# Output stage of a two-layer diffusion trunk: one buffer for each block's input, scaled ahead, and the gate row transposed ahead of the first products

## The chip, the core and the metric

The kernel runs on one core of one Trainium2 chip. The core has four engines that compute, TensorE (PE, matrix products and transposes), VectorE (DVE), ScalarE (ACT) and GpSimd (POOL), and a queue of SyncE (SP) from which this kernel issues its transfers. Each engine takes its instructions strictly in the order of its own queue and waits at one whose inputs or buffers are not ready. The metric is the time of one execution on the device in microseconds.

## The reference

Two post-norm layers run over 1024 latent tokens of width 1024, with 256 context tokens that share the weights. The first layer is windowed attention with sinks, the second neighbourhood attention on a 64-wide grid. Both end alike, and only the end of the second layer, for the latent tokens, is touched here:

```python
    y = (o * jax.nn.silu(g)) @ w_out
    ...
        h = layer_norm(DEEPNORM_ALPHA * h + gate[:, None, :] * y, ln_g[i], ln_b[i])
```

So for each token the attention output times its gate path goes through a 1024 x 1024 matrix; the row is multiplied by `gate` (one vector of 1024 for all tokens), added to the scaled input of the layer, and normalised over its 1024 values with weights `ln_g` and `ln_b`.

## The kernel before

Matrix products are made in three passes to keep float32 accuracy: each operand is split into a high and a low part, and high x high, high x low and low x high are summed (`out_part`, lines 451 to 453).

The output stage works through eight blocks of 128 tokens. A block's product has 8 steps of depth (`KT`) and two halves of 512 columns, each in a bank of PSUM of its own (`psone`, four banks in turn), so 48 products of 128x128 by 128x512. Blocks 0 and 1 have only their last step left when the stage begins: the first seven were put between the attention's last pieces of work. The last step uses `o7`, the output of the last head pair, which is ready only when the attention ends. The other seven steps read `og`, which the attention wrote to device memory and which is loaded again in four transfers a block (line 395, one buffer of three, two blocks ahead). Block 7 has its second half cut in two quarters, so that less is left to do behind the last product.

The layer's input was left in device memory by the first layer, normalised but without its weights (`zdd`). For each block `x` is loaded from it (line 1336, one buffer of three), and GpSimd multiplies it by `vecs[0]` (line 1340) and adds `vecs[1]` (line 1341): the first layer's `ln_g` and `ln_b`, each times ALPHA, made by GpSimd at the start of the stage (line 1331).

For each half of a block VectorE then multiplies the product by the gate row `g1` (line 1355, which also empties the PSUM bank), adds `x` (line 1356) and takes statistics (line 1357). For the block it combines them (line 459) and adds the epsilon (line 460); GpSimd raises that to the power -1/2 (line 461, one value per token); VectorE subtracts the mean and multiplies by `ln_g` (line 1362), then scales by the result of line 461 and adds `ln_b` (line 1364), and SP stores the block (line 1365). `z`, in which all this happens, has three buffers.

The gate row `g1` is needed in every partition. It lies as eight columns in `dcol`; `gate_rows` broadcasts and transposes them on TensorE (line 377, eight transposes) and copies the result out of PSUM on ScalarE (line 378). It is called once, behind block 0's products.

The order on each engine is not written by hand here. The kernel is written as a program, and a planner plays it through with costs of its own when it is built: an engine that is free takes, among the instructions whose inputs are ready by then, the one that stands first in the program. An instruction written later can so pass one that is written earlier but is not ready in the planner's reckoning. The order is then fixed; the chip's own times no longer change it. The planner also places the buffers. The output stage's buffers lie on memory that the attention used before, and each transfer into one waits until the attention's last use of that place.

Of the kernel before, what the change touches and what calls it, by code (L numbers as in the profile page):

```python
# [11 lines left out]
F32 = mybir.dt.float32  # L12
# [3 lines left out]
ALU = mybir.AluOpType  # L16
# [3 lines left out]
P = 128  # L20
D = 1024
# [61 lines left out]
def build(tc, i, out):  # L83
    nc = tc.nc
    mm = nc.tensor.matmul
    dma = nc.sync.dma_start
    es = ExitStack()

    def pool(name, side="left", **kw):
        st = ExitStack()  # L90
        p = st.enter_context(tc.tile_pool(name=name, bufs=1, side=side, reuse_waits="tile", **kw))
        return p, st
# [4 lines left out]
    def psbig(name):  # L97
        return ps.tile([P, 1024], F32, tag="big", bufs=2, name=name)

    def psone(name):  # L100
        return ps.tile([P, 512], F32, tag="one", bufs=4, name=name)
# [10 lines left out]
    dcol = cp.tile([P, 32, 2], F32, name="dcol")  # L112
# [8 lines left out]
    zdd = dr.tile([S, D], F32, name="zdd")  # L121
# [251 lines left out]
    def gate_rows(dst, src):  # L373

        pg = psbig("gate")
        for j in range(KT):
            nc.tensor.transpose(pg[:, j * P : (j + 1) * P], src[:, j : j + 1].to_broadcast([P, P]), ident)
        nc.scalar.copy(dst, pg)
# [9 lines left out]
    def ogs_load(b, alloc):  # L388

        o = []  # L390
        for k0 in range(0, KT - 1, 4):
            n = min(4, KT - 1 - k0)
            t = alloc(k0 // 4, n)
            for x in range(2):
                dma(f32(t[x]), ogs[k0 : k0 + n, x, :, b * P : (b + 1) * P].rearrange("k p t -> p k t"))
            o += [(t[0][:, k], t[1][:, k]) for k in range(n)]
        return o

    def og_home(pl, tag, bufs=1):

        t = pl.tile([P, 2, KT - 1, P], F32R, tag=tag, bufs=bufs, name="og")
        return lambda k, n: [t[:, x, 4 * k : 4 * k + n] for x in range(2)]
# [35 lines left out]
    def part_of(y, sl):  # L438

        if len(y) == 3 and sl.start == 768:  # L440
            return y[2][:, : sl.stop - sl.start]
        nh, c = sl.start // 512, sl.start // 512 * 512
        return y[nh][:, sl.start - c : sl.stop - c]

    def out_part(y, sl, o, w, kts):

        yy = part_of(y, sl)
        for kt in kts:
            h, l = o[kt]
            wh, wl = w.at(kt, sl)  # L450
            mm(yy, h, wh, start=kt == 0, stop=False)
            mm(yy, h, wl, start=False, stop=False)
            mm(yy, l, wh, start=False, stop=kt == KT - 1)

    def ln_stats(pl, st):

        mv = pl.tile([P, 2], F32, tag="mv", bufs=2, name="mv")
        rs = pl.tile([P, 2], F32, tag="rsd", bufs=2, name="rsd")
        nc.vector.bn_aggr(mv, st)  # L459
        nc.vector.tensor_scalar(rs[:, 0:1], mv[:, 1:2], EPS, None, ALU.add)  # L460
        nc.gpsimd.tensor_tensor(rs[:, 1:2], rs[:, 0:1], half, ALU.pow)  # L461
        return mv, rs
# [810 lines left out]
    def grid_rows(t, b):  # L1273

        return t.rearrange("(r c) d -> r c d", c=64)[:, 8 * b : 8 * b + 8, :]
# [49 lines left out]
    ob, ob_st = pool("outB", "left")  # L1325
    vecs = []
    for j in range(4):
# [3 lines left out]
            nc.gpsimd.tensor_scalar(t, t, ALPHA, 0.0, ALU.mult, ALU.add)  # L1331
        vecs.append(t)
    parts_of = {0: o0, 1: o1}
    for b in range(8):
        x = ob.tile([P, D], F32, tag="x", bufs=3, name="x")
        dma(x, grid_rows(zdd, b))  # L1336
        tok = slice(b * P, (b + 1) * P)
        if b < 6:
            parts_of[b + 2] = ogs_load(b + 2, og_home(ob, "og", 3))
        nc.gpsimd.tensor_tensor(x, x, vecs[0], ALU.mult)  # L1340
        nc.gpsimd.tensor_tensor(x, x, vecs[1], ALU.add)  # L1341
        y = [y0, y1][b] if b < 2 else [psone(f"yB{b}_{nh}") for nh in range(3 if b == 7 else 2)]
        pairs = parts_of.pop(b) + [(o7[:, 0, tok], o7[:, 1, tok])]

        cuts = (0, 512, 768, 1024) if b == 7 else (0, 512, D)
        parts = [slice(*c) for c in zip(cuts, cuts[1:])]
        for sl in parts:
            out_part(y, sl, pairs, woB, range(KT) if b > 1 else (KT - 1,))
        if b == 0:
            g1 = ob.tile([P, D], F32, name="g1")  # L1350
            gate_rows(g1, dcol[:, 24:32, 0])
        z = ob.tile([P, D], F32, tag="z", bufs=3, name="z")
        st = ob.tile([P, 3, 6], F32, tag="stat", bufs=2, name="stat")
        for j, sl in enumerate(parts):
            nc.vector.tensor_tensor(z[:, sl], part_of(y, sl), g1[:, sl], ALU.mult)  # L1355
            nc.vector.tensor_tensor(z[:, sl], z[:, sl], x[:, sl], ALU.add)  # L1356
            nc.vector.bn_stats(st[:, j, :], z[:, sl])  # L1357
        mv, rs = ln_stats(ob, st[:, : len(parts)])
        cuts = (0, 512, 1024) if b == 7 else (0, D)
        parts = [slice(*c) for c in zip(cuts, cuts[1:])]  # L1360
        for sl in parts:
            nc.vector.scalar_tensor_tensor(z[:, sl], z[:, sl], mv[:, 0:1], vecs[2][:, sl], ALU.subtract, ALU.mult)  # L1362
        for sl in parts:
            nc.vector.scalar_tensor_tensor(z[:, sl], z[:, sl], rs[:, 1:2], vecs[3][:, sl], ALU.mult, ALU.add)  # L1364
            dma(grid_rows(out, b)[:, :, sl], z[:, sl])
# [97 lines left out]
```

## Time and profile before

| what | us |
|---|---|
| median of 3 runs | 1425.7 (1424.68 to 1426.22) |
| profiled execution, its own time | 1422.99 |
| its span in the trace | 1421.2 |
| first L1355 of the output stage | 1341.86 |
| last product ends | 1410.30 |
| last L1364 ends | 1417.26 |

Times in the rows are microseconds from the span's start. A row of a queue gives the start, the duration, the engine, the line of the kernel, the operation, what is written from what (buffer numbers left out), shapes, and in brackets the idle time before it and what ended that. `xN` joins N instructions in sequence, and the duration is then that of all of them. A row of a group gives the number of instructions, then the sum in us, the mean in ns, and the idle time ahead. "SPq" is the queue of the transfers: its rows show the issuing, not the moving of the data.

### The profile page before, as it was taken

How to read it: one execution, taken by the hardware profiler on the slowest of the kernel's cores; microseconds unless marked ns; L12 is line 12 of the kernel's file. 1: busy time of each engine (PE TensorE's matmuls, PEld its weight loads, DVE VectorE, ACT ScalarE, POOL GpSimd, SP SyncE). 2: the span in 40 equal slices, each digit the busy share in tenths (PEclk: the TensorE clock that was granted, in tenths of full speed). 3: DMA queues.
4: the chain of work that ended last, by engine and by line, in shares of the span. 5: the costliest groups of instructions: out<-in, count | busy, mean ns of one | idle time of the engine just before them, and what ended most of it. 6: DMA issues, size and time to landing. Idle time of an engine off the chain costs nothing. (4 is left out here: it accounts for less than half of the span.)

```text
span 1421.2 us, 25164 instructions
## 1 busy us (share of the span) xinstructions
PE 1385.3 (97%) x8816; PEld 1215.2 (86%) x8816; DVE 980.0 (69%) x2220; ACT 731.4 (51%) x1560; POOL 626.2 (44%) x776
## 2 busy tenths in 40 slices
PE   8999999999999999999999999999999999999996
PEld 6988898888988888888898899888998899888885
DVE  4658887878888789566433766566665564659598
ACT  4337776676776778432222555454454454558200
POOL 0326676667666567233211333332233232325583
PEclk9999999999999999999999999999999999999998
DMA  9572114123222114443187575564555564476753
GB/s 377 181 224 85 54 57 126 53 79 92 79 73 64 57 60 146 127 135 133 62 260 218 156 214 165 143 189 137 179 150 172 150 185 146 137 209 185 181 149 107
DMA packets 128141, 202.39 MB, mean 142 GB/s; under 512 B 9744, under 2 KB 66448, under 8 KB 128016
## 3 DMA queue, kind: packets, MB, share of 16 engines
q1 hardware_dynamic: 127872, 200.78, 47.0%
q8 instruction: 70, 1.15, 0.3%
q14 instruction: 55, 0.45, 0.1%
q10 hardware_dynamic: 144, 0.01, 0.0%
HBM read 145.18 MB, written 55.57 MB: 141 GB/s over the span
## 5 line engine op out<-in xcount | busy, mean ns | idle before, releaser
L334 POOL TENSOR_SCALAR s_B<-s_B,rs_B 128x640 f32<-128x640 f32 (+1 forms) x128 | 103.2, 806 | 289.8 <-DVE rs_B L333 262.7
L212 PE MATMUL pj<-uBh,wh 128*128 128x512 f32 (+1 forms) x448 | 175.9, 393 | 0.0
L213 PE MATMUL pj<-uBl,wh 128*128 128x512 f32 (+1 forms) x448 | 170.3, 380 | 0.0
L214 PE MATMUL pj<-uBh,wl 128*128 128x512 f32 (+1 forms) x448 | 170.1, 380 | 0.0
L329 ACT ACTIVATE s_B<-s_B,m_B 128x640 f32<-128x640 f32 (+1 forms) x128 | 102.9, 804 | 126.1 <-DVE m_B L322 125.9
L329 ACT ACTIVATE s_A<-s_A,m_A 128x641 f32<-128x641 f32 (+2 forms) x160 | 119.5, 747 | 82.9 <-DVE m_A L322 60.1
L168 POOL TENSOR_TENSOR wl<-wr,wh 128x512 fp32r<-128x512 f32 x65 | 88.2, 1358 | 158.1 <-ACT wh L163 146.4
L334 POOL TENSOR_SCALAR s_A<-s_A,rs_A 128x640 f32<-128x640 f32 (+2 forms) x160 | 128.8, 805 | 65.0 <-DVE rs_A L333 58.9
L322 DVE CUSTOM_DVE_ANT_0 s_A<-S_A,msk,nsk 128x640 f32<-128x640 f32 (+2 forms) x160 | 123.5, 774 | 32.3 <-PE S_A L755 18.2
L347 DVE TENSOR_TENSOR pt_B<-T_B,pt_B 128x640 fp32r<-128x640 f32 (+1 forms) x128 | 100.9, 788 | 60.2 <-ACT pt_B L345 59.7
L212 PE MATMUL pj<-uAh,wh 128*128 128x512 f32 (+1 forms) x384 | 140.2, 365 | 0.8 <-DVE otmp L794 0.8
L213 PE MATMUL pj<-uAl,wh 128*128 128x512 f32 (+1 forms) x384 | 137.6, 358 | 0.0
L214 PE MATMUL pj<-uAh,wl 128*128 128x512 f32 (+1 forms) x384 | 137.2, 357 | 0.0
L347 DVE TENSOR_TENSOR ptl_A<-T_A,pth_A 128x640 fp32r<-128x640 f32 (+2 forms) x160 | 114.1, 713 | 16.8 <-PE pvA L783 10.5
L341 PE MATMUL T_A<-ident,s_A 128*128 128x128 f32 x672 | 100.9, 275 | 10.7 <-DVE m_A L322 5.3
L345 ACT CAST pt_B<-T_B 128x640 fp32r<-128x640 f32 (+1 forms) x128 | 84.4, 659 | 48.2 <-PE T_B L341 47.2
L341 PEld LDWEIGHTS T_A<-ident,s_A 128*128 128x128 f32 x672 | 77.3, 140 | 37.0 <-issue 10.1
L322 DVE CUSTOM_DVE_ANT_0 s_B<-S_B,bias 128x640 f32<-128x640 f32 (+1 forms) x128 | 100.2, 783 | 8.0 <-PE S_B L1092 7.0
L345 ACT CAST pth_A<-T_A 128x640 fp32r<-128x640 f32 (+2 forms) x160 | 96.3, 602 | 17.2 <-PE T_A L341 15.7
L214 PEld LDWEIGHTS pj<-uBh,wl 128*128 128x128 f32 x448 | 84.3, 188 | 16.6
L213 PEld LDWEIGHTS pj<-uBl,wh 128*128 128x128 f32 x448 | 84.7, 189 | 9.1
L341 PE MATMUL T_B<-ident,s_B 128*128 128x128 f32 x608 | 88.1, 274 | 4.2 <-DVE pt_B L347 2.3
(224 smaller groups left out, 3866.8 us busy)
## 6 DMA issues: line engine op xcount, KB each, us to landing
kB<-kdB SPq DMA_DIRECT2D x64, 320.0 KB, 5.4
gw<-in_wadaT SPq DMA_DIRECT2D x48, 256.0 KB, 2.8
vdB<-st SPq DMA_DIRECT2D x20, 512.0 KB, 3.6
vB<-vdB SPq DMA_DIRECT2D x16, 640.0 KB, 4.6
wada<-in_wadaC SPq DMA_DIRECT2D x16, 512.0 KB, 9.6
kdB<-st SPq DMA_DIRECT2D x16, 512.0 KB, 2.8
qdB<-st SPq DMA_DIRECT2D x16, 512.0 KB, 3.7
qB<-qdB SPq DMA_DIRECT2D x32, 256.0 KB, 4.8
```

The source lines that it names most:

```text
L168: e.tensor_tensor(lo, r, f32(hi), ALU.subtract)
L212: mm(pt[:, :n], hi[:, sl], rh, start=kt == 0, stop=False)
L213: mm(pt[:, :n], hi[:, sl], rl, start=False, stop=False)
L214: mm(pt[:, :n], lo[:, sl], rh, start=False, stop=kt == KT - 1)
L322: nc.vector.tensor_tensor_reduce(outp, sc, in1, scale, init if init is not None else 3e38, ALU.add, ALU.min, accum_out=s.m)
L329: nc.scalar.activation(s.t[:, :n], s.t[:, :n], AF.Exp, bias=s.m, scale=-1.0, accum_out=s.sum)
L334: nc.gpsimd.tensor_scalar(s.t[:, : s.w], s.t[:, : s.w], s.rs, 1.0, ALU.mult, ALU.mult)
L341: nc.tensor.transpose(tp[:, k * P : (k + 1) * P], s.t[:, src * P : (src + 1) * P], ident)
L345: nc.scalar.copy(pt.hi[:, :n, hl, :], tv)
L347: nc.vector.tensor_tensor(pt.lo[:, :n, hl, :], tv, f32(pt.hi[:, :n, hl, :]), ALU.subtract)
```

## The change

The eight `x` get a buffer each (32 KB a partition in place of 12). Loading and scaling are put in a function, `x_make`, which is called once ahead of block 0's `og` load, twice behind it, twice more in block 1, and once in each of blocks 2, 3 and 4. The loads of `x` no longer wait for a buffer, and in the program's order an `x` stands two or three blocks ahead of its use. The call of `gate_rows` moves from behind block 0's products to ahead of them.

```diff
     parts_of = {0: o0, 1: o1}
+    xs = []
+
+    def x_make():
+        x = ob.tile([P, D], F32, name=f"x{len(xs)}")
+        dma(x, grid_rows(zdd, len(xs)))
+        nc.gpsimd.tensor_tensor(x, x, vecs[0], ALU.mult)
+        nc.gpsimd.tensor_tensor(x, x, vecs[1], ALU.add)
+        xs.append(x)
+
     for b in range(8):
-        x = ob.tile([P, D], F32, tag="x", bufs=3, name="x")
-        dma(x, grid_rows(zdd, b))
         tok = slice(b * P, (b + 1) * P)
+        if b == 0:
+            x_make()
         if b < 6:
             parts_of[b + 2] = ogs_load(b + 2, og_home(ob, "og", 3))
-        nc.gpsimd.tensor_tensor(x, x, vecs[0], ALU.mult)
-        nc.gpsimd.tensor_tensor(x, x, vecs[1], ALU.add)
+        for _ in range(2 if b in (0, 1) else 1 if len(xs) < 8 else 0):
+            x_make()
+        x = xs[b]
...
+        if b == 0:
+
+            g1 = ob.tile([P, D], F32, name="g1")
+            gate_rows(g1, dcol[:, 24:32, 0])
         for sl in parts:
             out_part(y, sl, pairs, woB, range(KT) if b > 1 else (KT - 1,))
-        if b == 0:
-            g1 = ob.tile([P, D], F32, name="g1")
-            gate_rows(g1, dcol[:, 24:32, 0])
```

More of the change, by code (lines that the diff above doesn't have):

```diff
@@ L1346, in build @@
         parts = [slice(*c) for c in zip(cuts, cuts[1:])]
-        for sl in parts:
-            out_part(y, sl, pairs, woB, range(KT) if b > 1 else (KT - 1,))
         if b == 0:
@@ L1351, in build @@
             gate_rows(g1, dcol[:, 24:32, 0])
+        for sl in parts:
+            out_part(y, sl, pairs, woB, range(KT) if b > 1 else (KT - 1,))
         z = ob.tile([P, D], F32, tag="z", bufs=3, name="z")
```

## The prediction

> **What bounds the kernel now.** I read the head of the page first, then the groups of the last 80 us by form, then the queues of POOL, DVE, PE and SP in order of time.
>
> ```profile
> span 1421.2 us, 25164 instructions
> PE 1385.3 (97%) x8816; PEld 1215.2 (86%) x8816; DVE 980.0 (69%) x2220; ACT 731.4 (51%) x1560; POOL 626.2 (44%) x776
> ```
>
> PE is busy for 97% of the whole, but the change touches only the output stage, and there the end is set by another engine. These are rows of VectorE (start, duration, then the instruction):
>
> ```profile
> 1341.86 1.29 DVE L1355 TENSOR_TENSOR z<-yB,g 128x512 f32<-128x512 f32 x2 [10.04 <-ACT g L378]
> 1348.61 0.14 DVE L460 TENSOR_SCALAR rsd<-mv 128x1 f32<-128x1 f32 x1
> 1382.75 0.68 DVE L1355 TENSOR_TENSOR z<-yB,g 128x512 f32<-128x512 f32 x1
> 1392.74 0.68 DVE L1355 TENSOR_TENSOR z<-yB,g 128x512 f32<-128x512 f32 x1
> 1402.08 0.68 DVE L1355 TENSOR_TENSOR z<-yB,g 128x512 f32<-128x512 f32 x1
> 1409.53 0.69 DVE L1355 TENSOR_TENSOR z<-yB,g 128x512 f32<-128x512 f32 x1
> 1412.83 0.41 DVE L1355 TENSOR_TENSOR z<-yB,g 128x256 f32<-128x256 f32 x1
> 1415.85 1.41 DVE L1364 SCALAR_TENSOR_TENSOR z<-z,rsd,vec 128x512 f32<-128x512 f32 x2
> ```
>
> The first row is block 0. The next L1355 rows open blocks 4, 5, 6 and 7: block 4 takes 9.99 us, block 5 9.34, block 6 only 7.45. Now PE over the same stretch:
>
> ```profile
> 1338.35 0.40 PE L451 MATMUL yB<-woBh,o 128*128 128x512 f32 x1
> 1339.74 1.04 PE L377 MATMUL gate<-ident,dcol 128*128 128x128 f32 x8
> 1340.53 0.49 PE L451 MATMUL yB<-woBh,o 128*128 128x512 f32 x1
> 1342.61 0.50 PE L451 MATMUL yB<-woBh,og 128*128 128x512 f32 x1 [0.42 <-DVE z L1355]
> 1387.60 0.39 PE L451 MATMUL yB<-woBh,og 128*128 128x512 f32 x1
> 1410.02 0.28 PE L453 MATMUL yB<-woBh,o 128*128 128x256 f32 x1
> ```
>
> The last product ends at 1410.30, but VectorE takes it up only at 1412.83. So VectorE is **2.5 us behind** PE at the end and bounds the stage; if it kept up, the end would come at most 2.5 us earlier, and PE's own 0.42 us wait at 1342.61 (with 0.1 us in the longer product behind it) gives 0.5 more. **3.0 us is the most that anything here can win.**
>
> Why VectorE is behind is seen in its two-input instructions (ns: min/median/max):
>
> ```profile
> L1356 DVE TENSOR_TENSOR z<-z,x x17: 425/693/2884, 1343.1 to 1413.3; 128x512 f32<-128x512 f32 x15, 128x256 f32<-128x256 f32 x2
> L1362 DVE SCALAR_TENSOR_TENSOR z<-z,mv,vec x9: 740/1275/2269, 1348.7 to 1415.2; 128x1024 f32<-128x1024 f32 x7, 128x512 f32<-128x512 f32 x2
> L1364 DVE SCALAR_TENSOR_TENSOR z<-z,rsd,vec x9: 743/1285/3412, 1350.5 to 1416.5; 128x1024 f32<-128x1024 f32 x7, 128x512 f32<-128x512 f32 x2
> L1356 DVE TENSOR_TENSOR z<-z,x 128x512 f32<-128x512 f32 x15 | 21.1, 1413 | 0.3
> L1364 DVE SCALAR_TENSOR_TENSOR z<-z,rsd,vec 128x1024 f32<-128x1024 f32 x7 | 15.2, 2175 | 1.8 <-POOL rsd L461 1.8
> L1362 DVE SCALAR_TENSOR_TENSOR z<-z,mv,vec 128x1024 f32<-128x1024 f32 x7 | 10.9, 1557 | 0.0
> ```
>
> Mean against median: 15 x 0.72 + 7 x 0.89 + 7 x 0.28 = **19.0 us of stretching**. And POOL's queue shows with whom it collides:
>
> ```profile
> 1332.71 2.41 POOL L1340 TENSOR_TENSOR x<-x,vec 128x1024 f32<-128x1024 f32 x1
> 1335.19 2.40 POOL L1341 TENSOR_TENSOR x<-x,vec 128x1024 f32<-128x1024 f32 x1
> 1340.22 2.38 POOL L1340 TENSOR_TENSOR x<-x,vec 128x1024 f32<-128x1024 f32 x1 [2.64 <-DMA x<-zdd]
> 1342.68 2.40 POOL L1341 TENSOR_TENSOR x<-x,vec 128x1024 f32<-128x1024 f32 x1
> 1349.17 1.19 POOL L461 TENSOR_TENSOR rsd<-rsd,half 128x1 f32<-128x1 f32 x1 [4.09 <-PE yB L453]
> 1352.87 3.27 POOL L1341 TENSOR_TENSOR x<-x,vec 128x1024 f32<-128x1024 f32 x1
> 1356.10 2.86 POOL L1340 TENSOR_TENSOR x<-x,vec 128x1024 f32<-128x1024 f32 x1
> 1360.37 1.53 POOL L461 TENSOR_TENSOR rsd<-rsd,half 128x1 f32<-128x1 f32 x1 [1.41 <-DVE rsd L460]
> 1371.14 3.26 POOL L1341 TENSOR_TENSOR x<-x,vec 128x1024 f32<-128x1024 f32 x1
> 1374.36 2.85 POOL L1340 TENSOR_TENSOR x<-x,vec 128x1024 f32<-128x1024 f32 x1
> 1377.29 2.73 POOL L1341 TENSOR_TENSOR x<-x,vec 128x1024 f32<-128x1024 f32 x1
> 1379.99 1.53 POOL L461 TENSOR_TENSOR rsd<-rsd,half 128x1 f32<-128x1 f32 x1
> 1396.62 2.72 POOL L1341 TENSOR_TENSOR x<-x,vec 128x1024 f32<-128x1024 f32 x1
> ```
>
> L1340 is the multiply and L1341 the add on one x; L461 is the reciprocal root of a block, for which L1364 waits. Alone an x instruction takes 2.40 us; back to back beside VectorE it takes 2.7 to 3.3. From block 0's start to the add of x7 (1396.62), 13 x instructions run beside VectorE; 19.0 / 13 = 1.46 us of stretching each. Block 6, with none beside it, shows the bare 7.45 us.
>
> **The change, part by part.** (1) *The gate row.* The eight transposes move ahead of block 0's six products. Those took 1339.74 - 1338.35 = 1.39 us, so g and the first L1355 come 1.4 us earlier. But L1356 behind it needs the path that POOL occupies: at 1341.66 it meets x1's multiply (until 1342.60) and then its add, and the second L1356 ends near 1346.1, as now. Bounds 0 and -1.4; I take **-0.2**, since those rows of POOL stay where they are. PE's 0.5 us is gained but hidden while VectorE is the bound.
>
> (2) *The x loads.* SP's queue: two issues, two of its waits (us in total, times, longest), and the stretch from 1325 to 1342, whose last figure is GB/s:
>
> ```profile
> 1331.85 2.01 SPq L395 DMA_DIRECT2D og<-ogdB  x4
> 1333.90 0.54 SPq L1336 DMA_DIRECT2D x<-zdd  x1
> SPq L395 <- DVE o L1159: 8.8, 1, 8.8
> SPq L1336 <- DVE z L1356: 7.0, 3, 4.1
> 1325.00:1342.00 17.00, 17.00 (x89) 14.16 (x88) 2.97 (x6) 3.46 (x7) 11.94 (x10) 1.00 0.80 217
> ```
>
> With eight buffers the 7.0 us of waiting for an L1356 goes, and x3 to x7 are loaded without it. x2 passes four og transfers, and x3, x4 pass og of block 4. Up to that og SP moves three og of 0.92 MB and four x of 0.52 (by their shapes), 4.8 MB; at 217 GB/s that is 22 us from 1331.85, so 1354. Block 4 starts two blocks behind 1342.61; a block is 48 products at 0.232 us (six from 1338.35 to 1339.74), 11.1 us, so 1365. Covered by the products of blocks 2 and 3, cost 0; without those 11 us PE would wait that long. The larger pool lies on more of the attention's memory: og waits 8.8 us for its last instruction now, and x1 queues behind it. If x1 came free of this, it could be scaled at 1337.6 instead of 1340.22, and one instruction fewer would collide (-1.46); if another x takes over the place, nothing changes. Bounds -1.5 and 0; I take 0.
>
> (3) *POOL's order.* The instructions are the same sixteen. What moves is where they stand against the four or five early L461. x1 already goes ahead of block 0's L461, though written behind it, because it was loaded; x3's multiply goes ahead of block 1's, x4 and x5 ahead of block 3's. With every x loaded early, two more will stand ahead of each. POOL works in order, so L461 waits, and VectorE waits at L1364 with all its later work behind it.
>
> I follow POOL from the end of x1's add, 1345.08. x2's multiply ends at 1347.5; block 0's L461 (ready at 1348.75) ends at about 1350.0. Ahead of block 3's L461 then stand x2's add, x3 to x6 (8), none, one or both instructions of x7, and two L461 at 1.53. An x instruction back to back costs the mean of the five such rows (3.27, 2.86, 3.26, 2.85, 2.73: 2.99) and a gap of 0.08, **3.1 us**; bounds are 2.48 (alone, 1332.71 to 1335.19) and 2.40 + 1.28 = 3.7 (an L1364 in each gap). At 3.1, block 3's L461 starts at 1350.0 + 3.1 + (27.9, 31.0 or 34.1 less 3.1) + 3.1 = 1381.0, 1384.1 or 1387.2, against 1379.99 now: **1.0, 4.1 or 7.2 us late**. Afterwards blocks 4 and 5 run with fewer x beside them. They lie 2.54 and 1.89 above the bare 7.45, 4.4 together, 1.1 for each of their four x instructions. With two, one or none left, 2.2, 3.3 or 4.4 come back. The ends move by -1.2, +0.8 or +2.8, and with the gate row by **-1.4, +0.6 or +2.6**.
>
> Here a rule of the Trainium skill can be weighed (SBUF — State Buffer, "Who interferes with whom"): VectorE with two SBUF inputs and a GpSimd instruction that reads SBUF shut each other out for a whole instruction. The rows agree in kind (L1364 up to 3412 ns against 1285). Taken at its worst the rule gives an estimate of 12 x 2.40 = 28.8 us of waiting in place of 19.0, so +9.8; the rows say that VectorE spends part of each POOL instruction on L1355 and L1357, which are not stretched, and 1.46 us is left, so the rule's worst gets no chance of its own.
>
> I choose the middle one. In the trace an L461 falls between the two instructions of an x (x3 at block 1), and x7 is the last in the order of the program.
>
> The sum is made against the profiled execution, 1422.99 us, 1.79 above its span; the median of the runs shown is 1425.7, 2.7 above it. 1422.99 + 0.6 = 1423.6; against the median **1426.3**.
>
> **The rivals.**
>
> *VectorE catches up.* x1 free early, each L461 between two x, x instructions nearer 2.5 us: then VectorE is through with the collisions by block 4, takes the last product at once, and PE bounds. That gives the full 3.0: **1422.7**. For it: blocks 5 to 7 have no x at all beside them. Against: the number of collisions falls only from 13 to 12, and VectorE has no idle time in which to absorb them before block 4.
>
> *L461 behind all of x7* (the slower side). Place: block 3's L461. Its price: 11 instructions at the longest row, 3.27 + 0.08, are 36.9; 1350.0 + 36.9 + 3.1 = 1390.0, 10 us late; less 4.4 and 0.2, +5.4: **1431.1**. It decides from the point at which more comes late than blocks 4 and 5 give back, 4.4 us; nearly the same lateness (1387.60 - 1383.43 = 4.2 us for block 4's first half) is where PE starts to wait for the bank that L1355 empties. For it: x4 and x5 stand both ahead of block 3's L461 already. Against: x7's loads are the last ones.
>
> *The order of POOL hardly changes*, because the loads arrive as late as now (SP keeps 0.5 MB transfers behind og and the outputs). Then the gate row alone is left, -0.2: **1425.5**. Against: the wait for L1356 is named in the queue, and it goes.
>
> **How the numbers follow.** A measurement of this kernel can tell about 0.2% (2.9 us) from no change. Chances: the forecast with its two neighbours (1424.3 to 1428.3) 0.60; VectorE catches up 0.13; L461 behind all of x7 0.19; the order hardly changes 0.08. The 3.0 us limit leaves little room below 1422.9, and I cut the range there; the slow case is let in to 1429.6, about half of it. The likeliest case's own range is 1424.3 to 1428.3. Faster by over 0.2%: 0.13, nearly all of the first rival. Slower: 0.24, the second rival and the upper edge of the forecast. Within: 0.63.
>
> **What would show it.** Right: no "DMA x<-zdd" wait of L1340 after x2; x7's add ends before 1392 (now 1399.34); block 3's L1364 comes later than 1381.55, behind an L461 that starts the moment an x instruction ends; blocks 5 and 6 both at 7.4 to 7.5 us; stretching still 17 to 20 us in all. The gate row: L377 ahead of 1338.35 in PE's order, and no wait at the first product of block 2. Wrong, if VectorE's last L1355 follows the last product within 0.3 us (the first rival), if PE waits more than 1 us for L1355 (the second), or if the stretching falls below 14 us: then the collisions went and were not only moved.

## The result, and the profile after

The changed kernel takes **1426.8 us** (median of 22 runs, 1425.05 to 1429.81) against 1424.33 us for the kernel before (22 runs beside them, 1423.24 to 1427.15). The ratio is **1.0015, with an interval of 1.0009 to 1.0021**: 2.1 us slower (1.3 to 3.0), which is a real difference, but within the 0.2% that the prediction called no change. The prediction was 1426.3 us, 0.6 above before.

The profiled execution took 1425.88 us, its span 1424.1. A note for all that follows: the profiled execution of the kernel before (1422.99 us) is 1.3 us faster than its median of 1424.33, so a comparison with its trace can make another kernel look slower by up to that much. Verdicts come from the ratios, mechanisms from the traces.

VectorE's three two-input groups after the change (sum in us, mean in ns, then the idle time ahead):

```profile
L1368 DVE TENSOR_TENSOR z<-z,x 128x512 f32<-128x512 f32 x15 | 19.0, 1272 | 0.3
L1376 DVE SCALAR_TENSOR_TENSOR z<-z,rsd,vec 128x1024 f32<-128x1024 f32 x7 | 17.3, 2474 | 7.0 <-POOL rsd L461 7.0
L1374 DVE SCALAR_TENSOR_TENSOR z<-z,mv,vec 128x1024 f32<-128x1024 f32 x7 | 10.3, 1470 | 0.0
```

L1368, L1376 and L1374 are the L1356, L1364 and L1362 of before; L1367 is L1355, and L1377 the store. The stretching is hardly changed, but the wait for L461, 1.8 us before, is now 7.0. Where it lies is seen in VectorE's queue:

```profile
1330.45 0.94 DVE L1159 TENSOR_TENSOR o<-gB,o 128x256 fp32r<-128x256 f32 x1 [1.35 <-ACT o L1156]
1340.04 1.89 DVE L1367 TENSOR_TENSOR z<-yB,g 128x512 f32<-128x512 f32 x3 [8.65 <-ACT g L378]
...
1378.40 1.27 DVE L1374 SCALAR_TENSOR_TENSOR z<-z,mv,vec 128x1024 f32<-128x1024 f32 x1
1385.32 3.39 DVE L1376 SCALAR_TENSOR_TENSOR z<-z,rsd,vec 128x1024 f32<-128x1024 f32 x1 [5.64 <-POOL rsd L461]
1388.63 0.68 DVE L1367 TENSOR_TENSOR z<-yB,g 128x512 f32<-128x512 f32 x1
...
1397.52 0.68 DVE L1367 TENSOR_TENSOR z<-yB,g 128x512 f32<-128x512 f32 x1
...
1404.97 0.69 DVE L1367 TENSOR_TENSOR z<-yB,g 128x512 f32<-128x512 f32 x1
...
1412.42 0.69 DVE L1367 TENSOR_TENSOR z<-yB,g 128x512 f32<-128x512 f32 x1
...
1415.73 0.41 DVE L1367 TENSOR_TENSOR z<-yB,g 128x256 f32<-128x256 f32 x1
...
1418.75 1.41 DVE L1376 SCALAR_TENSOR_TENSOR z<-z,rsd,vec 128x512 f32<-128x512 f32 x2
```

Two rows of the kernel before belong beside these, its last L1159 and the L1364 of its block 3:

```profile
1330.88 0.95 DVE L1159 TENSOR_TENSOR o<-gB,o 128x256 fp32r<-128x256 f32 x1 [1.35 <-ACT o L1156]
...
1381.55 1.28 DVE L1364 SCALAR_TENSOR_TENSOR z<-z,rsd,vec 128x1024 f32<-128x1024 f32 x1 [0.44 <-POOL rsd L461]
```

I measure the stage from the end of the last L1159 to the end of the last long instruction. It took 1417.26 - 1331.83 = 85.43 us before and 1420.16 - 1331.39 = **88.77** after, 3.3 more. The account, block by block:

- The first product is taken up 1.4 us earlier (8.65 us of waiting in place of 10.04).
- In block 3 VectorE waits 5.64 us for L461 (0.44 before), and the L1376 behind it takes 3.39 us (1.28 before): +5.2 and +2.1. The rest up to block 4 adds 0.4. So block 4 begins 1388.63 - 1331.39 = 57.24 us into the stage in place of 50.92, **6.3 late**.
- Block 4 takes 8.89 us (9.99 before) and block 5 takes 7.45 (9.34): 3.0 come back. Blocks 6 and 7 are as before.

6.3 - 3.0 = 3.3. Now POOL, for whose L461 block 3 waits:

```profile
1369.01 2.39 POOL L1340 TENSOR_TENSOR x<-x,vec 128x1024 f32<-128x1024 f32 x1
1371.48 3.25 POOL L1341 TENSOR_TENSOR x<-x,vec 128x1024 f32<-128x1024 f32 x1
1379.93 2.38 POOL L1340 TENSOR_TENSOR x<-x,vec 128x1024 f32<-128x1024 f32 x1 [5.20 <-DMA x<-zdd]
1382.39 2.39 POOL L1341 TENSOR_TENSOR x<-x,vec 128x1024 f32<-128x1024 f32 x1
1384.74 0.55 POOL L461 TENSOR_TENSOR rsd<-rsd,half 128x1 f32<-128x1 f32 x1
1385.25 2.38 POOL L1340 TENSOR_TENSOR x<-x,vec 128x1024 f32<-128x1024 f32 x1
1387.71 3.23 POOL L1341 TENSOR_TENSOR x<-x,vec 128x1024 f32<-128x1024 f32 x1
```

These are x5, x6, block 3's L461 and x7. POOL stood 5.20 us at x6, whose data had not come, with block 3's small L461 queued behind it; it then scaled x6 and only at 1384.74 took the L461. In SP's queue x6's load is the third row, behind the store of block 2, which waits for that block's last instruction:

```profile
1366.39 3.62 SPq L395 DMA_DIRECT2D og<-ogdB  x4
1372.51 0.58 SPq L1377 DMA_DIRECT2D out_h<-z  x1
1373.13 0.60 SPq L1339 DMA_DIRECT2D x<-zdd  x1
```

And PE, with the view of one stretch behind it (its length, then busy time and number of instructions of PE, PEld, DVE, ACT and POOL, PE's granted clock, DMA share, GB/s):

```profile
1386.24 0.40 PE L453 MATMUL yB<-woBh,o 128*128 128x512 f32 x1
1389.37 0.50 PE L451 MATMUL yB<-woBh,og 128*128 128x512 f32 x1 [2.73 <-DVE z L1367]
...
1390.62 0.63 PE L452 MATMUL yB<-woBl,og 128*128 128x512 f32 x1
1391.05 0.63 PE L453 MATMUL yB<-woBh,og 128*128 128x512 f32 x1
...
1413.41 0.28 PE L453 MATMUL yB<-woBh,o 128*128 128x256 f32 x1
```

```profile
1389.30:1393.50 4.20, 4.13 (x11) 3.29 (x12) 4.10 (x5) 0.00 (x0) 1.63 (x1) 0.60 0.81 189
```

Because VectorE stands still, the bank of block 4's first half, which block 6 uses next, is not emptied, and PE waits 2.73 us at block 6's first product. Still PE isn't the bound at the end: its last product ends at 1413.69, and VectorE takes it at 1415.73, 2.0 us later.

### The profile page after: what moved, and what is told of

The parts are those of the page before. It is cut to its first block, busy times and chain, and to the rows that moved or that the text cites. A ratio compares the mean times of both kernels' runs of the same rounds, so it can differ in the third digit from the quotient of the medians.

```text
span 1424.1 us, 25163 instructions
## 1 busy us (share of the span) xinstructions
PE 1387.2 (97%) x8816; PEld 1216.2 (85%) x8816; DVE 979.9 (69%) x2220; ACT 731.0 (51%) x1560; POOL 626.3 (44%) x776
## 5 line engine op out<-in xcount | busy, mean ns | idle before, releaser
L212 PEld LDWEIGHTS pj<-uBh,wh 128*128 128x128 f32 x448 | 84.5, 189 | 9.0
```

The costliest lines, as they stand in the source:

```text
L212: mm(pt[:, :n], hi[:, sl], rh, start=kt == 0, stop=False)
```

## The experiments

The theory is that L461, one value per token, stands in POOL's queue behind whole x instructions, and VectorE behind L461. The rivals are that the late load of x6 is the cause, that the gate row's move is, or that PE's later end is. All ratios are to the kernel before on the same chip. "Stage" is as above; "wait" is VectorE's for the root in all; "stretching" is taken against the bare means of e5 (688, 1283 and 1276 ns).

| kernel | gate row ahead | x early | root on | ratio | stage | wait | stretching |
|---|---|---|---|---|---|---|---|
| before | no | no | POOL | 1 | 85.4 | 1.8 | 19.1 |
| after | yes | yes | POOL | 1.0015 [1.0009, 1.0021] | 88.8 | 7.0 | 18.5 |
| e1 | yes | no | POOL | 1.0007 [0.9998, 1.0015] | 87.1 | 4.0 | 19.8 |
| e2 | no | yes | POOL | 0.9993 [0.9984, 1.0002] | 84.5 | 4.0 | 15.9 |
| e3 | yes | earlier still | POOL | 1.0009 [1.0, 1.0017] | 87.8 | 6.6 | 16.5 |
| e4 | yes | x6, x7 behind the roots | POOL | 1.0006 [0.9997, 1.0015] | 86.9 | 1.8 | 21.8 |
| e5 | yes | loaded, not scaled | POOL | 0.9969 [0.9958, 0.998] | 82.2 | 2.2 | 0 |
| e6 | yes | yes | ScalarE | **0.9968 [0.9957, 0.998]** | 82.5 | 0.1 | 16.0 |
| e7 | no | yes | ScalarE | 0.9979 [0.997, 0.9987] | 84.9 | 0.1 | 19.0 |
| e8 | no | no | ScalarE | 0.9979 [0.997, 0.9988] | 84.6 | 0.1 | 18.8 |
| e9 | yes | no | ScalarE | 0.9978 [0.9969, 0.9987] | 83.5 | 0.1 | 18.9 |
| e10 | as e4 | as e4, a gap behind each root | POOL | 0.9978 [0.9967, 0.9988] | 83.2 | 4.0 | 15.8 |

In e3, e5 and e6 VectorE takes the last product within 0.04 us of its end, so there PE sets the end of the stage. In the other kernels VectorE is late at the end, and the columns add up. The stage differs from that of before by the change in waiting and the change in stretching, less 1.4 us where the gate row is ahead (the first product is taken up earlier), plus 1.2 us for eight reciprocals where the root is on ScalarE. This holds to within 0.3 us for each of them.

### The two halves of the change: e1 and e2

e1 is the kernel before with this edit alone:

```diff
+        if b == 0:
+
+            g1 = ob.tile([P, D], F32, name="g1")
+            gate_rows(g1, dcol[:, 24:32, 0])
         for sl in parts:
             out_part(y, sl, pairs, woB, range(KT) if b > 1 else (KT - 1,))
-        if b == 0:
-            g1 = ob.tile([P, D], F32, name="g1")
-            gate_rows(g1, dcol[:, 24:32, 0])
```

> The kernel before with the gate row alone moved ahead of block 0's products. Theory (the gate row's 1.4 us are lost again on POOL): g copied by about 1340.4 in place of 1341.8, but the two L1356 of block 0 still end near 1346, so the time against before is 0.9995 to 1.0003. Rival (VectorE bounds the stage from its first instruction on, so an earlier start is kept to the end): 1.4 us less, 0.999.

e2 is the changed kernel with that edit undone:

> The changed kernel with the gate row back behind block 0's products: buffers and early scaling alone. Theory (the added time is the wait of block 3's L1376 for an L461 that stands behind x6 on POOL): it is as long as POOL lets it be; the planner puts x6's load one output earlier in SP's queue here, so x6 is there in time and the wait falls from 5.6 to 1 to 3 us, ratio 0.9995 to 1.001. Rival (the early scaling itself costs, by collisions): as the change, 1.0015.

Measured: e1 1426.7 us, 1.0007, its stage 1.7 longer than before; e2 1425.36 us, 0.9993, its stage 0.9 shorter. Neither is told from no change by its ratio, and neither alone makes the 88.8 us. e1 lies above both of its expectations (1.0003 at most). e2 lies just below its range, and the wait that was expected to fall to 1 to 3 us is down to 0.44. The planner plays the whole program through, so moving eight transposes also moved other work. In e1 the load of x3 went behind the store of block 0, and these are its waits (us in all, times, longest). The 2.2 us is VectorE's wait in block 2, whose L461 stands behind both instructions of the late x3:

```profile
POOL rsd L461 <- DVE rsd L460: 17.4, 4, 6.5
POOL x L1340 <- DMA x<-zdd: 10.7, 4, 4.0
...
DVE z L1365 <- POOL rsd L461: 4.0, 5, 2.2
```

In e2 x6's load stands ahead of block 2's store, and block 3's long instruction waits no longer than it did before (of the 4.0 us in the table, 2.2 lie in block 1):

```profile
1383.86 1.29 DVE L1375 SCALAR_TENSOR_TENSOR z<-z,rsd,vec 128x1024 f32<-128x1024 f32 x1 [0.44 <-POOL rsd L461]
```

In e1 too it waits only 0.44 us. So the 5.6 us wait is made by the two parts together, through the order that results.

### Is it the late load? e3

The changed kernel with x5, x6 and x7 made in block 2, so that their loads stand ahead of that store:

```diff
-        for _ in range(2 if b in (0, 1) else 1 if len(xs) < 8 else 0):
+        for _ in range(2 if b in (0, 1) else 3 if b == 2 else 0):
             x_make()
```

> The changed kernel with x5, x6 and x7 all made in block 2, so that their loads stand ahead of more of SP's queue. Two theories of the 5.6 us wait of block 3's L1376. Late load (POOL stood 5.2 us at x6's multiply for its transfer): the transfer is there by 1374, block 3's L461 starts near 1379 and the time falls by 4 to 5 us, ratio 0.998. POOL's order (whatever stands ahead of L461 delays it): x6 and x7, four instructions, now stand ahead of it and it starts at 1386 to 1388, later than the 1384.7 of the change; afterwards no x collides any more, so the end comes 0 to 2 us earlier than the change's, ratio 1.000 to 1.0015.

Measured: 1426.95 us, 1.0009, about as the changed kernel. The wait for x6's data is gone, but POOL now has x6 and x7 ahead of block 3's L461:

```profile
1376.93 2.79 POOL L1340 TENSOR_TENSOR x<-x,vec 128x1024 f32<-128x1024 f32 x1
1379.80 2.69 POOL L1341 TENSOR_TENSOR x<-x,vec 128x1024 f32<-128x1024 f32 x1
1382.45 3.36 POOL L1340 TENSOR_TENSOR x<-x,vec 128x1024 f32<-128x1024 f32 x1
1385.89 2.39 POOL L1341 TENSOR_TENSOR x<-x,vec 128x1024 f32<-128x1024 f32 x1
1388.23 0.55 POOL L461 TENSOR_TENSOR rsd<-rsd,half 128x1 f32<-128x1 f32 x1
```

VectorE waits 5.24 us there:

```profile
1388.82 1.28 DVE L1376 SCALAR_TENSOR_TENSOR z<-z,rsd,vec 128x1024 f32<-128x1024 f32 x1 [5.24 <-POOL rsd L461]
...
1416.99 0.42 DVE L1367 TENSOR_TENSOR z<-yB,g 128x256 f32<-128x256 f32 x1 [1.23 <-PE yB L453]
```

Whether the time ahead of L461 is a missing load or more scaling makes little difference to this wait: it is the place in the order that counts. The time of e3 doesn't settle it, since PE sets its end. An `og` came late there (2.57 and 0.92 us of waiting on PE), and as the second row shows, VectorE waited 1.23 us for the last product.

### The order undone: e4, and why it won so little

x6 and x7 are made at the end of blocks 3 and 4 and may be issued only behind the root of those blocks (the list `powers` holds the roots; the lines that fill it are left out here):

```diff
...
-        nc.gpsimd.tensor_tensor(x, x, vecs[0], ALU.mult)
-        nc.gpsimd.tensor_tensor(x, x, vecs[1], ALU.add)
+        with tc.issue_after(powers[len(xs) - 3]) if len(xs) >= 6 else nullcontext():
+            nc.gpsimd.tensor_tensor(x, x, vecs[0], ALU.mult)
+            nc.gpsimd.tensor_tensor(x, x, vecs[1], ALU.add)
...
-        for _ in range(2 if b in (0, 1) else 1 if len(xs) < 8 else 0):
+        for _ in range(2 if b in (0, 1) else 1 if b == 2 else 0):
             x_make()
...
+        if b in (3, 4):
+            x_make()
```

> The changed kernel with the two instructions of x6 put behind block 3's L461 on POOL, and those of x7 behind block 4's. Theory (L461 behind x6 is what costs): the wait of block 3's L1376 falls from 5.6 to about 0.5 us, PE's wait of 2.7 us goes, and the end comes 4 to 5 us earlier than the change's, 1.5 to 2 us earlier than before's: ratio 0.9985 to 0.999. Rival (collisions only moved, and VectorE's total is what it is): the same sixteen instructions collide with the same work, the time stays at 1.001 to 1.002.

Measured: 1425.69 us, 1.0006, between the ranges of the two. The long wait is gone as expected (1.8 us in all), but the stage is only 1.8 us shorter than the changed kernel's, less than I expected: stretching is up from 18.5 to 21.8 us. The two queues show why. The last instructions of blocks 3 and 4 are, with what stands behind the root on POOL:

```profile
1381.48 3.41 DVE L1382 SCALAR_TENSOR_TENSOR z<-z,rsd,vec 128x1024 f32<-128x1024 f32 x1 [0.44 <-POOL rsd L463]
...
1392.54 3.42 DVE L1382 SCALAR_TENSOR_TENSOR z<-z,rsd,vec 128x1024 f32<-128x1024 f32 x1 [0.44 <-POOL rsd L463]
```

```profile
1379.93 1.52 POOL L463 TENSOR_TENSOR rsd<-rsd,half 128x1 f32<-128x1 f32 x1 [3.83 <-DVE rsd L462]
1381.42 2.39 POOL L1344 TENSOR_TENSOR x<-x,vec 128x1024 f32<-128x1024 f32 x1
```

The x instruction behind the root starts 0.06 us ahead of the VectorE instruction that the root releases, and that one then takes 3.4 us in place of 1.28. In the kernel before, x6 and x7 waited for their loads at these places, by the same view, so VectorE went first:

```profile
1382.98 2.40 POOL L1340 TENSOR_TENSOR x<-x,vec 128x1024 f32<-128x1024 f32 x1 [1.46 <-DMA x<-zdd]
...
1394.15 2.39 POOL L1340 TENSOR_TENSOR x<-x,vec 128x1024 f32<-128x1024 f32 x1 [2.65 <-DMA x<-zdd]
```

### Who starts first: e10

If 0.06 us decide, a short delay on POOL must turn it round. e10 is e4 with a second root, whose result nothing uses, behind each:

```diff
-        powers.append(nc.gpsimd.tensor_tensor(rs[:, 1:2], rs[:, 0:1], half, ALU.pow).ins)
+        nc.gpsimd.tensor_tensor(rs[:, 1:2], rs[:, 0:1], half, ALU.pow)
+        aft = pl.tile([P, 1], F32, tag="aft", bufs=2, name="aft")
+        powers.append(nc.gpsimd.tensor_tensor(aft, rs[:, 0:1], half, ALU.pow).ins)
```

> The kernel of e4_behind_power with one more root of 128 elements (its result unused) on POOL directly behind each of the eight, so that an x instruction that stands behind a root starts about 0.5 us later. Theory (the first of the two to start has the path for its whole length, and in e4 x6 and x7 started 0.06 us ahead of VectorE's last instruction of the block): in the blocks where VectorE waits for the root, 3 and 4, that instruction falls from 3.4 to 1.28 us, and the x instruction behind the root starts at its end, or starts on time and shows some 1.3 us more; stage 1 to 4 us below e4's 86.9, ratio 0.998 to 1.0. Rival (POOL's long instruction gets in ahead whichever starts first): the instruction stays at 3.4 us, and the stage is 0 to 2 us above e4's.

Measured: 1422.57 us, **0.9978 [0.9967, 0.9988]**, clear of e4's interval and of no change, with 18 more instructions on POOL (`ln_stats` also serves the first layer, so ten of them lie ahead of this stage). The stage is 83.2, 3.7 under e4's. The group of the long instruction shows no stretching at all:

```profile
L1384 DVE SCALAR_TENSOR_TENSOR z<-z,rsd,vec 128x1024 f32<-128x1024 f32 x7 | 9.0, 1283 | 4.0 <-POOL rsd L463 4.0
```

```profile
1381.27 1.28 DVE L1384 SCALAR_TENSOR_TENSOR z<-z,rsd,vec 128x1024 f32<-128x1024 f32 x1 [0.44 <-POOL rsd L463]
1381.21 0.54 POOL L465 TENSOR_TENSOR aft<-rsd,half 128x1 f32<-128x1 f32 x1
1381.72 3.10 POOL L1346 TENSOR_TENSOR x<-x,vec 128x1024 f32<-128x1024 f32 x1
```

POOL's instruction now carries the delay (3.10 us in place of 2.39), and it is off the critical path. The same is seen in blocks 0 to 2: in block 2, for example, POOL starts at 1370.36 and VectorE at 1370.50 in e4 (3.33 us), but VectorE at 1371.60 and POOL at 1371.97 in e10 (1.27 us). The stretching falls from 21.8 to 15.8 us for the same sixteen instructions, and 2.2 us of it go into more waiting for the root: the sum is not fixed by how many instructions collide, but depends on who goes first. The Trainium skill (SBUF — State Buffer, "Who interferes with whom") says that issue order, not the shape of the operation, decides who blocks, and these rows agree: 3.41 against 1.28 us for the same instruction.

### How much the collisions cost: e5

The changed kernel without lines 1340 and 1341:

> The changed kernel without its two x instructions (x is loaded and added unscaled, so the output lacks the factor ALPHA*vec0 and the offset ALPHA*vec1 on x). My theory (collisions with POOL's x instructions are the whole of VectorE's lag): the stretching of VectorE's three two-input groups falls from 18.4 us to under 2, every block of VectorE runs at 7.4 to 7.5, VectorE catches up with PE before the last block and takes the last product within 0.5 us of its end; the stage (end of the last L1159 to the end of the last L1376) comes to 82 to 83.5 us against 85.4 before and 88.8 after: ratio to the kernel before 0.997 to 0.9985. Rival (PE's late end is the bound of the changed kernel, since its last product ends at 1413.7 against 1410.3): PE still ends as late, and the stage stays above 87 us, ratio over 1.000.

Measured: 1421.54 us, 0.9969, stage 82.2. From 1366 us on VectorE waits for PE in each block, 15.2 us in all, and takes the last product 0.04 us after its end. That is the floor that PE sets, 3.2 under the traced stage before, where the prediction's limit was 3.0.

### The root off POOL: e6 to e9

The root is made by ScalarE (square root) and VectorE (reciprocal, behind the first long instruction), so POOL holds nothing but the x instructions:

```diff
-        mv, rs = ln_stats(ob, st[:, : len(parts)])
+        mv = ob.tile([P, 2], F32, tag="mv", bufs=2, name="mv")
+        rs = ob.tile([P, 2], F32, tag="rsd", bufs=2, name="rsd")
+        nc.vector.bn_aggr(mv, st[:, : len(parts)])
+        nc.vector.tensor_scalar(rs[:, 0:1], mv[:, 1:2], EPS, None, ALU.add)
+        nc.scalar.activation(rs[:, 0:1], rs[:, 0:1], AF.Sqrt)
...
             nc.vector.scalar_tensor_tensor(z[:, sl], z[:, sl], mv[:, 0:1], vecs[2][:, sl], ALU.subtract, ALU.mult)
+        nc.vector.reciprocal(rs[:, 1:2], rs[:, 0:1])
```

On the changed kernel:

> The changed kernel with the reciprocal root of the eight output blocks taken off POOL: a square root on ScalarE and a reciprocal on VectorE behind the first of the two long instructions. POOL then holds nothing but the sixteen x instructions. Theory 1 (the changed kernel loses because L461 stands behind x6 in POOL's order): no wait of VectorE for POOL is left; a wait for ScalarE of 0 to 0.5 us per block and 0.1 us of reciprocal cost 1 to 4 us in all; stretching stays 16 to 19 us. The stage comes to 83 to 86 us, ratio 0.997 to 0.9995: 3 to 5 us under the changed kernel. Theory 2 (what L461 waits for is only moved: the x instructions that no longer wait collide as often, and the time comes back as stretching): stretching over 21 us and the ratio at 1.000 to 1.0015.

Measured: **1420.8 us, 0.9968 [0.9957, 0.998]**, as fast as e5, which does no scaling at all, and better than both kernels: 4.6 us under before (2.9 to 6.1). Stage and ratio are a little better than the theory's ranges. POOL still waits for the load of x5, 8.2 us, and for others, 9.3 in all; with no root behind it, that costs nothing:

```profile
POOL x L1340 <- DMA x<-zdd: 9.3, 3, 8.2
DVE z L1367 <- ACT g L378: 8.7, 1, 8.7
```

```profile
1396.94 0.15 DVE L1379 RECIPROCAL rsd<-rsd 128x1 f32<-128x1 f32 x1
1397.13 1.28 DVE L1381 SCALAR_TENSOR_TENSOR z<-z,rsd,vec 128x1024 f32<-128x1024 f32 x1
...
1410.74 0.42 DVE L1367 TENSOR_TENSOR z<-yB,g 128x256 f32<-128x256 f32 x1 [1.50 <-PE yB L453]
```

The last row answers the sign that the prediction named: VectorE waits for the last product and takes it at once. Theory 2, that the time would come back as stretching, falls: stretching is 16.0 us.

The same on e2, on the kernel before and on e1:

> The same, with the gate row behind the first block's products as in the kernel before (x loads early, no POOL root). Theory (gate row is worth 0 to 1.4 us at the start, and costs only by the orders it changed around L461): without L461 on POOL it is 0 to 1.4 us slower than the same kernel with the gate row ahead, ratio 0.998 to 1.0. Rival (gate row itself makes the end later): faster than it by 1 us or more.

> The kernel before with the root of the output blocks taken off POOL in the same way. Theory (before, L461 cost VectorE only 1.8 us of waiting, so there is little to win; x loads stay late, and x instructions run beside VectorE until the end): ratio 0.9985 to 1.001, at least 1 us above the changed kernel with the same root, because the early x loads then pay. Rival (the root on POOL is the whole matter and the early loads pay nothing): equal to the changed kernel with the same root within 0.5 us.

> The kernel before with the gate row ahead of the first block's products and the root off POOL, the x loads as before (three buffers). With e6, e7, e8 it completes the square of gate row and x loads without a root on POOL (stages 82.5 with both, 84.9 with the x loads alone, 84.6 with neither). Theory A (the gate row is worth its 1.4 to 2.4 us once no root stands behind an x instruction, and the early loads pay nothing): stage 82.3 to 83.3 us, ratio 0.9965 to 0.998. Theory B (only both together pay: the late loads keep the x instructions beside VectorE until the last block): stage 84.0 to 85.0, ratio 0.9978 to 0.999.

Measured: 1422.86, 1422.87 and 1422.41 us, ratios 0.9979, 0.9979 and 0.9978. e7 is 1.6 us slower than e6 by the ratios, just outside the 0 to 1.4 expected. e8 missed its expectation: taking the root off POOL is worth 3 us (1.7 to 4.3) on the kernel before too, though VectorE had waited only 1.8 us for it. Its traced stage is only 0.8 us shorter, which is what its parts give (1.7 less waiting, 0.3 less stretching, 1.2 for the reciprocals); where the rest of the 3 us comes from stays open. By the stages, without a root on POOL the gate row is worth 2.4 us with early loads (84.9 to 82.5) and 1.1 without (84.6 to 83.5); early loads are worth 1.1 with the gate row and nothing without it. e6 stands at PE's floor, so the two figures against it could not come out larger. e9's 83.5 lies between its two theories, nearer to the first. By the ratios e6 is ahead of e7, e8 and e9 by 0.1%, which the intervals don't tell apart.

## Why the prediction was right, and which of its steps were not

The direction and the place (block 3's L461, given back in blocks 4 and 5) were right, and the time lies in the range. The size was forecast low: +0.6, with the slower neighbour at +2.6, against +2.1 measured (1.3 to 3.0). That 1426.3 came so near to 1426.8 is in part luck, because the median of before that it was added to, 1425.7 from 3 runs, stands 1.4 us above that of the 22. Step by step:

- **VectorE bounds the stage, and 3.0 us is all there is to win.** Right in the trace: with the collisions gone (e5) the stage falls by 3.2, with the root moved (e6) by 3.0, and PE then bounds. By the times both won over 4, but their intervals reach down to 2.9, so the times don't speak against the limit.
- **Stretching stays at 17 to 20 us.** Right for the change: by the prediction's own reckoning 15 x 0.58 + 7 x 1.19 + 7 x 0.20 = 18.4. The reason behind it, 1.46 us for each x instruction, was wrong: e4 and e10 have the same sixteen instructions and 21.8 against 15.8.
- **The gate row: -0.2, bounds -1.4 and 0.** The start did come 1.4 us earlier, and in the changed kernel it was lost again in block 0: the second L1368 ends 14.3 us into the stage, the second L1356 before 14.4. But the reason, "those rows of POOL stay where they are", failed. x1's multiply went from 1340.22 to 1337.45, and x2's, at 1342.25, took its place. Alone, in e1, the gate row makes the stage 1.7 slower, outside the bounds, by the order that came with it. The term belongs with that order, and can't be priced by itself.
- **The x loads cost nothing; no DMA wait after x2.** Right for `og`, for which PE never waits, and for x1, which came free early and left its place to x2. Wrong for the rest: x6 waited 5.20 us for its load, queued behind block 2's store. The sum had the bytes right and left out what stands ahead of a load in SP's queue and waits.
- **Block 3's L461 is 4.1 us late.** It is 4.75 late (1384.74 against 1379.99), but made up otherwise: nine x instructions ahead of it, not ten, which by the prediction was the 1.0 case, and the wait for x6 on top. That the two come so near is luck. The price of an x instruction was sound: e3 has all eleven ahead, the 7.2 case, and counted from the stage's start its L461 is 6.4 us later than before (54.56 against 48.16).
- **What was left out of that step:** L1376 behind the late root, 3.39 us for 1.28, since x7 started first. That 2.1 us is most of the 2.7 between the forecast's +0.6 and the trace's +3.3.
- **3.3 us come back in blocks 4 and 5.** 3.0 did. The add of x7 ends at 1390.94, and blocks 5 and 6 are both 7.45, as foretold.
- **"PE waits more than 1 us" as the sign of the slowest rival** was a poor sign. PE did wait 2.73 us, and eight products behind it ran slow, but 2.0 us of slack were left at the end; the rival's 1431.1 did not come.
- **The first rival, VectorE catching up,** didn't happen in the changed kernel, but is what e6 does, from one further edit.

## What to carry to other kernels

A small instruction that another engine waits for should not share an in-order queue with long ones that nobody needs yet: giving long work more freedom to run ahead also lets it stand ahead of the small one. Moving the small one to an idle engine turned a loss of 2.1 us into a gain of 4.6. Where two engines share a path, see which of them starts first after a common release: here that order alone took the stretching from 21.8 to 15.8 us. And where a planner sets the order, a part of a change has no price of its own; read the order that comes out.

## What the runs showed of the hardware that was not expected

- **0.06 us decide over 2.1 us.** POOL's next queued instruction starts right behind the root (1381.42) and ahead of the VectorE instruction that the root releases (1381.48); half a microsecond of unneeded work between them reverses it.
- **PE can pay twice for a wait.** After the 2.73 us wait of the changed kernel, the granted clock over the next 4.2 us is 0.60, and products come every 0.43 us in place of 0.23, for eight of them: about 1.5 us more. In e3, too, eight products come at that pace behind the waits of 2.57 and 0.92 us. After the 0.42 us wait before the change only one product was longer. The Trainium skill (TensorE: Matmul & The Clock Gate, "Part 1: The HAM clock gate") gives about 3.4 us for an idle window, which runs freely; here the slow products followed a wait of 2.73 us.
